# Decoder layer in f32 on one core: each full weight chunk is requested as two transfers of 512 KB instead of one of 1 MB

## The chip, the cores and the metric

The kernel runs on one core of a Trainium2 chip. The metric is the device time of one execution in microseconds (us), as the median of several executions. The kernel before took 1955.75 us (three executions, 1953.15 to 1957.33 us).

The core has five engines that run their own instruction streams side by side: TensorE (PE in the profile; PEld is its weight load), VectorE (DVE), ScalarE (ACT), GpSimd (POOL) and SyncE (SP), which here only asks for transfers. Each engine takes its instructions in the order in which they were placed, and waits at an instruction until the semaphores that it names have been reached. A transfer is issued by an instruction on an engine's queue (SP's queue is SPq in the profile), is carried out by 16 DMA engines, and reports its landing on a semaphore.

## The reference

One decoder layer on 256 tokens of width 2048, batch 1, everything in float32:

```python
hn = rmsnorm(h, norm_mix_w[l])
q, k, v, g_ret, xr, yr, g_a, g_b = jnp.split(hn @ w_in[l], offsets, axis=-1)
...
ret_out = jax.nn.silu(g_ret) * ret          # retention, 8 heads, rotary, head norm
rnn_out = jax.nn.gelu(yr) * hr              # causal conv of 4 taps, gated recurrence
merged = (jax.nn.sigmoid(g_a) * (ret_out @ w_proj_ret[l])
          + jax.nn.sigmoid(g_b) * (rnn_out @ w_proj_rnn[l]))
h = h + merged @ w_mix_out[l]
hn = rmsnorm(h, norm_xa_w[l])
mem_n = rmsnorm(mem, norm_mem_w[l])
h = h + memory_cross_attention(hn, mem_n, xa_w_q[l], xa_w_k[l], xa_w_v[l], xa_w_o[l])
hn = rmsnorm(h, norm_ffn_w[l])
h = h + conv_gated_ffn(hn, ffn_w_up[l], ffn_conv_w[l], ffn_conv_b[l], ffn_w_down[l])
return rmsnorm(h, final_norm_w)
```

Nearly all of the work is in the products with the weight matrices: `w_in` is 2048 x 14336, seven more (both mixers' outputs, the merge, and four of the cross-attention) are 2048 x 2048, `ffn_w_up` is 2048 x 11264 and `ffn_w_down` is 5632 x 2048. Each weight is used once for the 256 tokens, so all of them have to be read from the chip's memory once per execution.

## The kernel before

**Products.** A float32 product is made of three products in the reduced type fp32r: a number is split into a high part (its value cast to fp32r) and a low part (the rest), and high x high, high x low and low x high are added up. So each weight has to be split on the chip. ScalarE casts (`hi`, line 451) and VectorE subtracts (`lo`, line 452), both in `weight_parts`, for two pieces of 128 x 512 at a time (`KH` = 2). TensorE then multiplies (line 285, every product of the kernel goes through this helper). The activations are the stationary operand, and the weights are streamed past them.

**Chunks.** The weights lie in one array `wall` in the order in which they are used, packed by the host so that what one partition needs of a chunk is contiguous. A full chunk is four pieces, 128 x 2048 numbers, 1 MB, 8 KB for each of the 128 partitions. There are two sorts of them that matter here:

- plain chunks: `for k in range(0, nk, KH): parts += weight_parts(raw[:, one])`. The first cast reads pieces 0 and 1, the second reads pieces 2 and 3.
- seven-part chunks (`seven_parts`, line 466): two column blocks are multiplied with seven products in the place of eight, from sums and differences of the four pieces. Their first cast reads `raw[:, 0:3:2]`, pieces 0 and 2, and their second reads piece 3. Line 473 then makes three sums over the pieces in place (VectorE), and two more pairs of casts and subtractions follow.

**Staging.** A generator (`chunks`) hands out the chunks in order and calls `prefetch` ahead of use (`AHEAD` = 2). `prefetch` takes the next entry of the stream, takes a tile `raw` of the pool with `RAW_BUFS` = 3 slots of 1 MB, asks for the load on SP's queue (line 416, which calls `load`, whose transfer is recorded as line 256), and lists the casts and subtractions. `hi` and `lo` have `PART_BUFS` = 6 slots of two pieces each, three chunks' worth. A load into a `raw` slot waits until the chunk three earlier has been read for the last time, which is a `lo` subtraction on VectorE.

Some chunks take other ways: the first six (small, at the start), those whose low part is made by a DMA that adds (`fr`, `fl`), and those of which a part comes in as `tw`.

**Order.** A scheduler places the instructions of all engines by priorities and its own estimates of durations; TensorE's products are held in program order (`keep_in_program_order`). SP's queue carries, beside the weight loads, 128 transposes by DMA (line 665 in `by_dma`, `pt<-pl`). For them ScalarE first splits rows into two planes (`pl`, line 664), and later joins the turned planes (`f`, line 677). On SP's queue a load that stands behind transposes is issued after them.

**Names that the text uses.** `raw`: a loaded chunk. `pl`, `pt`, `f`: planes before and after the turn, and the joined rows. `acc`, `sm`: sums in PSUM, `o`: sums that VectorE carries on (lines 627 and 638). `s`, `ts`: split activations. `fg`, `fv`, `ft`, `fo`: gate, value and their product in the FFN (lines 1280, 1282, 1290, 1291).

Of the kernel before, what the change touches and what calls it, by code (L numbers as in the profile page):

```python
# [30 lines left out]
KH = 2  # L31
# [168 lines left out]
def hybrid_layer(  # L200
# [155 lines left out]
    def prefetch(n):  # L356
        while len(ahead) < n and taken[0] < len(stream):
            i = taken[0]
            name, row, nk, c = stream[i]
# [48 lines left out]
            k2 = row // (KH * P)  # L408
            early = i < 2 * len(EARLY)
            own = early and i % 2 == 0  # L410
            cuts = () if i == 0 else range(0, nk + 1, KH) if i < 6 else (0, nk)
            if own:
                xs.load(k2 + 1)
            for a, b in zip(cuts, cuts[1:]):
# [69 lines left out]
    def chunks(nk, w, row, c):  # L484

        i = gemms[0]
        assert plan[i] == (w, row, nk, c), (i, w, row, nk, c)
        gemms[0] += 1
        for k, n in pieces(i, nk, c):
            prefetch(1)  # L490
            (r_, c_), parts = ahead.pop(0)
            assert (r_, c_) == (row + k * P, kind_of(c, k))
            prefetch(AHEAD)
            yield k, n, parts
            step[0] += 1
            due = [p for p in pending if p[0] <= step[0]]
            pending[:] = [p for p in pending if p[0] > step[0]]
            for _, fn in due:
                fn()
# [981 lines left out]
```

## Time and profile before

| what | value |
|---|---|
| median of three executions | 1955.75 us (1953.15 to 1957.33) |
| the profiled execution, its own time | 1956.59 us |
| span in its trace, first to last instruction | 1954.5 us |
| instructions on all engines in the trace | 24287 |
| TensorE clock granted, mean | 0.999 |
| weight loads of 1 MB on SP's queue | 319 |
| weight loads of 768 KB / of 512 KB into `raw` | 24 / 13 |
| transposes on SP's queue | 128 |
| DMA traffic | 454.99 MB, mean 233 GB/s |

The span is the time on the core, and the execution's own time is 2.1 us more. A row of the timeline names the start and the length of a run of like instructions, the engine, the line, and the tile written and read (`hi<-raw`). Its length goes from the first's start to the last's end. Instructions that only issue a transfer are not counted as busy work of an engine, but the queue's own rows (SPq) show how long each issue held the queue. "us to landing" counts from the issue to the semaphore that reports the transfer.

### The profile page before, as it was taken

To read this page: it belongs to the slowest core of one execution; us is meant where nothing else is said; L and a number is where in the kernel's file an instruction comes from. 1 tells how busy PE (TensorE), PEld (TensorE's weight loads), DVE (VectorE), ACT (ScalarE), POOL (GpSimd) and SP (SyncE) were. 2 spreads that over 40 slices of the span, in tenths; PEclk is the share of its full clock that TensorE was granted. 3 is DMA by queue.
4 is the path that set the end of the run, shared out by engine and by line. 5 is a ranking of instruction groups with operands and counts; after the bars stand their busy time and mean duration, and the time that the engine had idled before them with its cause. 6 is when DMAs were issued, how large, how long until landed. Compare 5 with 4: busy or idle time off the path is not lost.

```text
span 1954.5 us, 24287 instructions
## 1 busy us (share of the span) xinstructions
PE 1944.4 (99%) x8735; PEld 1612.9 (83%) x8735; DVE 1659.0 (85%) x2155; ACT 1457.7 (75%) x1792; POOL 68.5 (4%) x69
## 2 busy tenths in 40 slices
PE   9999999999999999999999999999999999999998
PEld 7888888888888888888888888888887888888887
DVE  6887987787889988887888857789999889999986
ACT  6665758999756666778678777888877578884784
POOL 0000001000100000000000000000000000000000
PEclk9999999999999999999999999999999999999999
DMA  8866767666867786778868687676677877678773
GB/s 332 262 215 198 245 222 217 213 218 229 237 217 265 233 264 215 253 253 252 247 213 239 223 221 225 226 232 226 211 224 224 269 248 221 223 224 271 230 255 119
DMA packets 211352, 454.99 MB, mean 233 GB/s; under 512 B 143264, under 2 KB 147872, under 8 KB 170400
## 3 DMA queue, kind: packets, MB, share of 16 engines
q1 hardware_dynamic: 204896, 430.38, 66.5%
q0 software_dynamic: 6336, 23.07, 6.3%
q8 instruction: 68, 1.11, 0.2%
q14 instruction: 52, 0.43, 0.1%
HBM read 407.27 MB, written 2.10 MB: 209 GB/s over the span
## 4 chain that ended last, share of the span: by engine, by line
PE 88%; DVE 5%; ACT 3%; DMA 2%; issue 2%; POOL 0%; SPq 0%; POOLq 0%; DVEq 0%; ACTq 0%
PE acc L285 63%; PE sm L285 26%; DVE lo L452 2%; ACT hi L451 1%; DMA raw<-in_wall 1%; ACT f L677 1%; DVE o L627 1%; ACT pl L664 0%; DMA fl<-fr 0%; DVE o L638 0%; DMA pt<-pl 0%; DVE raw L473 0%; DVE fv L1282 0%; DVE fg L1282 0%; DVE s L702 0%
## 5 line engine op out<-in xcount | busy, mean ns | idle before, releaser
L452 DVE TENSOR_TENSOR lo<-raw,hi 128x1024 fp32r<-128x1024 f32 (+1 forms) x824 | 940.4, 1169 | 203.0 <-ACT hi L451 193.0
L285 PE MATMUL acc<-hi,s 128*128 128x512 f32 x3526 | 1081.5, 388 | 0.4 <-ACT s L727 0.2
L451 ACT CAST hi<-raw 128x1024 fp32r<-128x1024 f32 (+1 forms) x824 | 801.1, 1007 | 301.9 <-DMA raw<-in_wall 83.1
L285 PEld LDWEIGHTS acc<-hi,s 128*128 128x128 f32 x3526 | 659.5, 188 | 136.1 <-DVE s L728 0.6
L285 PE MATMUL acc<-lo,s 128*128 128x512 f32 x1727 | 669.7, 388 | 0.1
L285 PE MATMUL sm<-hi,s 128*128 128x512 f32 x1464 | 450.9, 389 | 0.0
L285 PEld LDWEIGHTS acc<-lo,s 128*128 128x128 f32 x1727 | 324.4, 188 | 68.6 <-DVE lo L452 2.1
L285 PEld LDWEIGHTS sm<-hi,s 128*128 128x128 f32 x1464 | 274.7, 188 | 57.2 <-ACT prob L1203 0.2
L285 PE MATMUL sm<-lo,s 128*128 128x512 f32 x720 | 280.3, 389 | 0.0
L677 ACT COPY f<-pt 128x1024 uint16<-128x1024 uint16 x128 | 166.8, 1353 | 10.0 <-DMA pt<-pl 10.0
L285 PEld LDWEIGHTS sm<-lo,s 128*128 128x128 f32 x720 | 135.2, 188 | 28.6 <-DVE lo L452 0.6
L285 PE MATMUL acc<-hi,ts 128*128 128x512 f32 x438 | 134.9, 389 | 0.0
L473 DVE TENSOR_TENSOR raw<-raw 128x1024 f32<-128x1024 f32 x147 | 127.1, 865 | 1.9
L285 PEld LDWEIGHTS acc<-hi,ts 128*128 128x128 f32 x438 | 82.2, 188 | 17.0
L285 PE MATMUL acc<-lo,ts 128*128 128x512 f32 x219 | 85.7, 391 | 0.7 <-DVE lo L452 0.6
L664 ACT COPY pl<-o 128x1024 uint16<-128x1024 uint16 x64 | 62.5, 1040 | 3.7 <-DVE o L638 2.8
L330 POOL DMA_DIRECT2D tw<-in_wall x24 | 21.4, 891 | 980.8 <-DMA tw<-in_wall 355.7
L285 PEld LDWEIGHTS acc<-lo,ts 128*128 128x128 f32 x219 | 41.1, 188 | 10.8 <-DVE lo L452 2.4
L664 ACT COPY pl<-rows 128x1024 uint16<-128x1024 uint16 x44 | 43.7, 1044 | 7.6 <-DVE rows L694 7.6
L1421 ACT ACTIVATE o<-o,ro 128x512 f32<-128x512 f32 x44 | 30.1, 718 | 23.9 <-DVE o L638 23.8
L638 DVE TENSOR_TENSOR o<-o,sm 128x512 f32<-128x512 f32 x64 | 42.2, 679 | 3.9 <-PE sm L285 3.9
L285 PE MATMUL sm<-hi,ts 128*128 128x512 f32 x146 | 45.0, 389 | 0.0
(197 smaller groups left out, 1321.2 us busy)
## 6 DMA issues: line engine op xcount, KB each, us to landing
raw<-in_wall SPq DMA_DIRECT2D x319, 1024.0 KB, 5.1
raw<-in_wall SPq DMA_DIRECT2D x24, 768.0 KB, 5.6
tw<-in_wall SPq DMA_DIRECT2D x24, 512.0 KB, 7.7
tw<-in_wall POOLq DMA_DIRECT2D x24, 512.0 KB, 7.3
raw<-in_wall SPq DMA_DIRECT2D x13, 512.0 KB, 6.6
fr<-in_wall SPq DMA_DIRECT2D x12, 512.0 KB, 7.4
fl<-fr POOLq DMA_DIRECT2D x12, 512.0 KB, 8.1
nat<-in_x SPq DMA_DIRECT2D x8, 512.0 KB, 9.7
```

Of the source, the lines that this page charges most:

```text
L285: tc.keep_in_program_order(pe.matmul(*a, **k))
L330: pool.dma_start(out=far[i], in_=source(i)[:, 0:KH, :], accum_op=ALU.add)
L451: act.copy(hi[:, cs], src[:, cs])
L452: dve.tensor_tensor(out=lo[:, cs], in0=src[:, cs], in1=hi[:, cs].bitcast(F32), op=ALU.subtract)
L473: dve.tensor_tensor(out=o, in0=a, in1=b, op=ALU.add)
L627: dve.tensor_tensor(out=o, in0=a, in1=b, op=op)
L638: dve.tensor_tensor(out=o, in0=o, in1=a, op=ALU.add)
L664: act.copy(planes[:, tt], words[:, tt])
L677: act.copy(halves_[:, :, :, cs], turned_[:, :, :, cs])
L1421: act.mul(a[:, tt, :], a[:, tt, :], rs2[:, tt : tt + 1])
```

## The change

```diff
@@ prefetch
-            cuts = () if i == 0 else range(0, nk + 1, KH) if i < 6 else (0, nk)
+            cuts = () if i == 0 else range(0, nk + 1, KH)
             if own:
                 xs.load(k2 + 1)
             for a, b in zip(cuts, cuts[1:]):
                 with tc.issue_after(behind[-1]) if i in in_order else nullcontext():
                     load(raw[:, a:b, :], src[:, a:b, :], early)
```

`cuts` are the pieces at which a chunk's load is cut. From the seventh entry of the stream on they were (0, 4), and are now 0, 2, 4 as for the first ones: pieces 0 and 1 in one transfer, pieces 2 and 3 in a second one, into the two halves of the same tile, 4 KB for each partition in each. The bytes, the tiles, the casts and the products are the same. On SP's queue there are 885 transfer instructions in the place of 566, 319 more. PE's and POOL's order is the same row for row. The scheduler places some rows of the others differently; all but 20 of the pairs stand back to back on SP's queue. Three places follow. Numbers in names differ between the two kernels, since names are counted through.

SP's queue in the FFN, at chunk A, a seven-part chunk (`raw_13903` before, `raw_14168` now). Before:

```order
L256 DMA raw_13869<-in_wall 128x2048
L256 DMA raw_13903<-in_wall 128x2048
L665 DMA_TRANSPOSE pt_13806<-pl_13805 128x8x128 x2
L665 DMA_TRANSPOSE pt_13814<-pl_13813 128x8x128 x2
L256 DMA raw_13956<-in_wall 128x2048
```

Now:

```order
L256 DMA raw_14133<-in_wall 128x1024 x2
L256 DMA raw_14168<-in_wall 128x1024
L665 DMA_TRANSPOSE pt_14070<-pl_14069 128x8x128 x2
L665 DMA_TRANSPOSE pt_14078<-pl_14077 128x8x128 x2
L256 DMA raw_14168<-in_wall 128x1024
L256 DMA raw_14222<-in_wall 128x1024 x2
```

The load of A stood whole ahead of the four transposes. Its first half still does; its second half stands behind them. Eight chunks on, at chunk B (`raw_14264` before, `raw_14537` now, also of seven parts), SP's queue has the same pattern.

ScalarE at chunk B (`f` and `fg` are the FFN's joined rows and gate, `ft` its activation). Before:

```order
L451 CAST hi_14266<-raw_14264 128x1024
L677 COPY f_14309<-pt_14178 128x2x4x128
L451 CAST hi_14270<-raw_14264 128x512
L677 COPY f_14309<-pt_14178 128x2x4x128
L1280 ACTIVATE fg_13819<-f_14309,pf 128x256 x2
L451 CAST hi_14277<-raw_14264 128x1024
L1280 ACTIVATE fg_13819<-f_14309,pf 128x256 x2
L677 COPY f_14402<-pt_14186 128x2x4x128
L451 CAST hi_14281<-raw_14264 128x1024
```

Now:

```order
L677 COPY f_14583<-pt_14449 128x2x4x128 x2
L1280 ACTIVATE fg_14083<-f_14583,pf 128x256 x3
L451 CAST hi_14540<-raw_14537 128x1024
L451 CAST hi_14544<-raw_14537 128x512
L1280 ACTIVATE fg_14083<-f_14583,pf 128x256
L677 COPY f_14678<-pt_14457 128x2x4x128 x2
L1290 ACTIVATE ft_14687<-fg_14083 128x512
L451 CAST hi_14551<-raw_14537 128x1024
L1280 ACTIVATE fv_14084<-f_14678,pf 128x256 x2
L451 CAST hi_14555<-raw_14537 128x1024
```

The two joins of `f` and three of the gate's rows moved ahead of B's first cast, and the joins of the next planes and `ft` ahead of its third.

VectorE at chunk C, a plain chunk of the FFN (`raw_12362` before, `raw_12595` now). Before:

```order
L1282 SCALAR_TENSOR_TENSOR fv_11711<-f_12295,pf,fv_11711 128x254
L452 TENSOR_TENSOR lo_12365<-raw_12362,hi_12364 128x1024
L638 TENSOR_TENSOR o_12343<-o_12343,sm_12085 128x512
L1291 TENSOR_TENSOR fo_12356<-ft_12355,fv_11711 128x512
L638 TENSOR_TENSOR o_12343<-o_12343,sm_12086 128x512
L452 TENSOR_TENSOR lo_12369<-raw_12362,hi_12368 128x1024
```

Now:

```order
L1282 SCALAR_TENSOR_TENSOR fv_11930<-f_12527,pf,fv_11930 128x254
L638 TENSOR_TENSOR o_12576<-o_12576,sm_12312 128x512
L638 TENSOR_TENSOR o_12576<-o_12576,sm_12313 128x512
L1291 TENSOR_TENSOR fo_12589<-ft_12588,fv_11930 128x512
L452 TENSOR_TENSOR lo_12599<-raw_12595,hi_12598 128x1024
L452 TENSOR_TENSOR lo_12603<-raw_12595,hi_12602 128x1024
```

C's first subtraction stood ahead of two sums of `o` and the product `fo`, and now stands behind all three.

## The prediction

> **What bounds the kernel now.** I read the page first: the shares of the engines, the DMA queue, and the chain that ended last.
>
> ```profile
> span 1954.5 us, 24287 instructions
> PE 1944.4 (99%) x8735; PEld 1612.9 (83%) x8735; DVE 1659.0 (85%) x2155; ACT 1457.7 (75%) x1792; POOL 68.5 (4%) x69
> q1 hardware_dynamic: 204896, 430.38, 66.5%
> PE 88%; DVE 5%; ACT 3%; DMA 2%; issue 2%; POOL 0%; SPq 0%; POOLq 0%; DVEq 0%; ACTq 0%
> ```
>
> TensorE is busy in 1944.4 of 1954.5 us, and the loads fill the 16 DMA engines to 66.5%. Then the busy time by stretches, to see where TensorE's missing 10.1 us lie. The columns are the length, then for PE, PEld, DVE, ACT and POOL the busy time with the number of instructions, then clock, DMA share and GB/s.
>
> ```profile
> 0.00:14.00 14.00, 12.71 (x49) 9.88 (x50) 7.54 (x17) 8.00 (x15) 0.97 (x7) 1.00 0.84 299
> 14.00:1420.00 1406.00, 1405.24 (x6341) 1167.99 (x6340) 1177.29 (x1527) 1066.71 (x1313) 53.02 (x44) 1.00 0.73 234
> 1420.00:1540.00 120.00, 119.15 (x518) 96.42 (x517) 108.06 (x137) 86.92 (x106) 3.52 (x4) 1.00 0.77 240
> 1540.00:1946.00 406.00, 406.00 (x1822) 337.55 (x1822) 363.87 (x469) 294.90 (x360) 10.43 (x13) 1.00 0.71 228
> 1946.00:1954.50 8.50, 1.32 (x12) 1.11 (x10) 2.26 (x7) 1.12 (x2) 0.54 (x1) 0.85 0.35 135
> ```
>
> The start (1.29 us, with chunks that the change leaves as they are) and the tail (7.18 us, after the last product) hold 8.47 us of it. Between them, in 1932 us, TensorE stands still for 0.76 + 0.85 + 0.00 = 1.61 us. So an earlier load has next to nothing to win, and whatever holds TensorE up once is paid in full. The question is whether TensorE is ever made to wait, and this hangs on the staging ahead of it. The waits, by who waited for whom (total us, times, longest):
>
> ```profile
> ACT hi L451 <- DMA raw<-in_wall: 83.1, 63, 5.7
> ACT hi L451 <- PE acc L285: 77.6, 73, 3.1
> ACT hi L451 <- PE sm L285: 57.5, 61, 1.9
> SPq L256 <- DVE lo L452: 1209.9, 300, 11.9
> PE acc L285 <- DVE lo L452: 0.6, 2, 0.4
> ```
>
> ScalarE waits for a load 63 times and for TensorE (to free a `hi`) 134 times, while TensorE waited only twice, for 0.6 us, for a subtraction. The staging is ahead nearly everywhere, by little. SP's queue waits 1209.9 us for VectorE to free a `raw` slot.
>
> **The change part by part.** *The 319 further issues.* The first row gives what one issue holds the queue (least, median, most, in ns); the others are page rows and single issues in the trace (KB, us to landing).
>
> ```profile
> L256 SPq DMA_DIRECT2D raw<-in_wall x356: 327/328/1059, 1.7 to 1917.7; - x178
> raw<-in_wall SPq DMA_DIRECT2D x319, 1024.0 KB, 5.1
> raw<-in_wall SPq DMA_DIRECT2D x13, 512.0 KB, 6.6
> raw<-in_wall SPq DMA_DIRECT2D x1, 512.0 KB, 3.1
> raw<-in_wall SPq DMA_DIRECT2D x1, 1024.0 KB, 4.7
> raw<-in_wall SPq DMA_DIRECT2D x2, 1024.0 KB, 6.0
> ```
>
> 319 x 0.33 = 105 us of SP's time, in a queue that waits 1209.9 us for slots: hidden where nothing urgent stands behind it. Without that cover it would delay the second half by 0.33 us per chunk, and ScalarE's wait with it.
>
> *Landing.* The third and second rows from the end are one load of 512 KB (issued at 523.0) and one of 1 MB (1631.7), each without another weight load in flight: 3.1 and 4.7 us. (The last row is two loads asked for between 1684.2 and 1685.4, of use further down.) So a first half lands up to 1.6 us sooner, and a second half, issued 0.33 us later, at about the old time. The median over 13 loads of 512 KB (they come amid other transfers) is 6.6 us, more than the 5.1 us of the full ones, so neither order of sizes is safe: I bound a half's landing by 3.1 and 6.6 us and take 4.0 us amid transposes, nearer the lone row. For plain chunks, whose first cast needs the first half only, part of the 83.1 us of ScalarE's waits goes. TensorE gets from it at most its own pauses. A pause looks shorter in busy time than it is, since a product is counted 0.39 us but the next one starts 0.23 us after it; I double the 1.61 us: a gain between 0 and 3.2 us. I take 0.5, as TensorE's waits in the list end at VectorE.
>
> [...]
>
> *Chunk A.* Its second half now stands behind four transposes on SP's queue. Before (start, length):
>
> ```profile
> 1635.19 0.33 SPq L256 DMA_DIRECT2D raw<-in_wall  x1
> 1635.57 8.36 SPq L665 DMA_TRANSPOSE pt<-pl  x4
> 1644.03 1.68 SPq L256 DMA_DIRECT2D raw<-in_wall  x2
> ...
> 1639.30 4.42 ACT L451 CAST hi<-raw 128x1024 fp32r<-128x1024 f32 x5 [0.28 <-DVE raw L337]
> 1647.73 1.04 ACT L451 CAST hi<-raw 128x1024 fp32r<-128x1024 f32 x1
> ...
> 1645.53 1.22 DVE L473 TENSOR_TENSOR raw<-raw 128x1024 f32<-128x1024 f32 x1
> 1648.87 1.22 DVE L452 TENSOR_TENSOR lo<-raw,hi 128x1024 fp32r<-128x1024 f32 x1
> ...
> 1652.93 0.62 PE L285 MATMUL acc<-hi,ts 128*128 128x512 f32 x2
> 1653.38 0.39 PE L285 MATMUL acc<-lo,ts 128*128 128x512 f32 x1
> ```
>
> The half is issued at 1635.57 + 8.36 = 1643.9 in the place of 1635.2, and lands at 1647.9 (1647.0 to 1650.5). A is of seven parts, so its first cast needs both halves: it moves from about 1642 (the fourth of the five casts at 1639.30) to 1647.9. From there the order is cast (1.04 us), subtraction and the three sums of line 473. Before, 3.3 us lay between the first sum's start (1645.53) and the third subtraction's (1648.87). First subtraction at about 1648.9, first sum some 1.8 us later at 1650.7, third subtraction at 1654.0, done at 1655.2. TensorE reads it at 1653.38: **1.8 us late, I take 2** (0 by the early landing and the sums closer together, 4 by the late one).
>
> *Chunk B*, the same pattern eight chunks on, and the chunk behind it:
>
> ```profile
> 1676.18 0.33 SPq L256 DMA_DIRECT2D raw<-in_wall  x1
> 1676.56 7.63 SPq L665 DMA_TRANSPOSE pt<-pl  x4
> ...
> 1681.70 1.05 ACT L451 CAST hi<-raw 128x1024 fp32r<-128x1024 f32 x1 [0.38 <-DMA raw<-in_wall]
> 1692.63 1.04 ACT L451 CAST hi<-raw 128x1024 fp32r<-128x1024 f32 x1
> ...
> 1700.63 3.50 DVE L452 TENSOR_TENSOR lo<-raw,hi 128x1024 fp32r<-128x1024 f32 x3
> ...
> 1702.34 0.39 PE L285 MATMUL acc<-lo,ts 128*128 128x512 f32 x1
> ```
>
> The second half is issued at 1684.2 and lands at 1688.2, so B's first cast moves by 6.5 us from 1681.70. The new order on ScalarE (shown with the change) uses part of that time: both joins and three gate rows stand ahead of it now. What is left between B's first cast and the next chunk's (10.9 us before) I add up at 7.9 us, so the next chunk's first cast starts at 1696.1 in the place of 1692.63, 3.5 us late. It had no spare time: its fourth subtraction, at 1700.63, was done at 1701.8 for a product at 1702.34. Some VectorE rows (`fv`) no longer stand between, worth about 1 us, and 0.5 us was spare: **2 us** (0 to 4; should the transposes' own delays shift PE's need by A's stall, less).
>
> *Chunk C* moves by the scheduler alone. Its first subtraction now stands behind two sums and `fo`:
>
> ```profile
> 1458.47 1.21 DVE L452 TENSOR_TENSOR lo<-raw,hi 128x1024 fp32r<-128x1024 f32 x1
> 1459.61 0.68 DVE L638 TENSOR_TENSOR o<-o,sm 128x512 f32<-128x512 f32 x1
> ...
> 1461.41 1.21 DVE L452 TENSOR_TENSOR lo<-raw,hi 128x1024 fp32r<-128x1024 f32 x1
> ...
> 1458.99 0.61 PE L285 MATMUL acc<-hi,s 128*128 128x512 f32 x2
> 1459.74 0.50 PE L285 MATMUL acc<-lo,s 128*128 128x512 f32 x1
> ```
>
> The three rows took 1461.41 - 1459.61 = 1.80 us. TensorE was already waiting for this subtraction: two products further on it starts 0.75 us after 1458.99, where two rows above (1652.93 to 1653.38) it takes 0.45. So nearly all 1.8 us reach it; the subtractions behind it are then less pressed, which may give back some of the pauses after it. **1.5 us** (0 to 1.9).
>
> *The other 18 pairs that are pulled apart*, and rows moved by a few places on ScalarE and VectorE. Most pairs stand in stretches where ScalarE waits for TensorE, with spare time of some us; a plain chunk needs its second half only for its second cast. Each could cost between nothing and A's 4 us. **1 us** for all (0 to 6).
>
> The sum against the profiled execution's own 1956.6 us: 2 + 2 + 1.5 + 1 - 0.5 = +6.0, so 1962.6. That execution lies 0.8 us above the median of the three shown; against the median, **1962 us**. The bounds add to -3.2 and +16, not all likely at once.
>
> **The rivals.** *One: nothing of it reaches TensorE* (not slower). The mechanism is the spare time at A, B and C: if the second halves land 3.1 us after issue, with the sums of line 473 following at once, A's third subtraction is done in time, and the scheduler's other moves give back at C what they take. For it: TensorE's two short waits in the old trace and the 134 times at which ScalarE waits for it. It decides once the delays at A and B stay below 6 us together with the shorter work between. Against it: the spare time of 0.5 us behind B and of none at C. It gives 1955 to 1958 us. *Two: faster,* by the earlier first halves alone: TensorE's pauses of up to 3.2 us go and A to C cost nothing, 1956.6 - 3.2 - 0.8 = 1952.6 us. For it, ScalarE's 63 waits for loads and VectorE's waits behind them; against it, C's pause, which ends at VectorE's row above it. *Three: the two halves of a chunk follow each other instead of overlapping,* so that a chunk takes 2 x 3.1 = 6.2 us in the place of 4.7. ScalarE's 63 waits for loads grow by 1.5 us each, 95 us, of which I let a quarter reach TensorE, as it has spare time at most places: +24, 1980 us. Against it: two full loads asked for within 1.2 us landed after 6.0 us (the median of both), where in turn the second would have needed some 9. *Four: more of the 18 pairs than I think strike,* at 2 us each for five of them: +10, some 1970 us.
>
> **How the numbers follow.** A measurement of this kernel tells about 0.2% from no change, 3.9 us: faster means below 1951.8, slower above 1959.7. My forecast (delays at A, B, C, +4 to +8) has a chance of 0.50, rival one 0.22, two 0.12, three 0.05, four 0.11. Rival two lies 0.8 us above the border and the three runs shown lie 4 us apart, so faster gets half of it, 0.06; the same gets one, the other half of two and 0.06 of the forecast whose stalls fall short, 0.34; slower the rest, 0.44 + 0.05 + 0.11 = 0.60. For the range, 8 in 10: from 1954, which takes in rival one and leaves out two, to 1971, which takes in most of rival four and leaves out three. The forecast's own range is 1959 to 1966.
>
> **What would show it.** In the new trace: transfers of 512 KB, some 640 of them, and landings of about 3 to 4 us. At A, SP's queue holds the four transposes between two issues of `raw`, and TensorE pauses about 2 us, in the timeline some 18 us after the first half's issue, ending at `lo<-raw`. After B a second such pause ends at `lo`; at C one of 1.5 us. TensorE's waits for `lo` rise from 0.6 to 5 or 6 us, and nothing ends at a DMA directly. The sum of ScalarE's waits for `raw` may fall for the plain chunks. I would be wrong if TensorE's idle time stays below 3 us outside start and tail, if it pauses at many chunks whose halves stand back to back (rival three), or if the largest pauses lie at pairs that I did not price.

## The result: 1972.05 us, 0.85% slower, and the profile after

| | median | ratio to the kernel before |
|---|---|---|
| before, beside it | 1955.12 us (1953.15 to 1957.33, 4 runs) | |
| both halves asked for apart | 1972.05 us (1970.71 to 1972.73, 4 runs) | 1.0085 (95% interval 1.0072 to 1.0098) |
| predicted | 1962.0 us (range 1954 to 1971) | |

The direction was right and the size was not: 17 us in the place of 6, and just outside the range. The page of the kernel after, the rows that answer to those shown of before:

```profile
span 1970.8 us, 24888 instructions
PE 1949.9 (99%) x8735; PEld 1612.3 (82%) x8735; DVE 1658.6 (84%) x2155; ACT 1457.7 (74%) x1792; POOL 70.0 (4%) x69
q1 hardware_dynamic: 250832, 430.40, 68.5%
raw<-in_wall SPq DMA_DIRECT2D x651, 512.0 KB, 4.9
```

The five engines have as many instructions as before, and the DMA engines are 2 points busier, with 45,936 further packets. A half lands after 4.9 us by the median, a whole load after 5.1. Busy time by stretches, with the same columns as before:

```profile
14.00:1420.00 1406.00, 1401.95 (x6318) 1162.79 (x6317) 1170.83 (x1516) 1060.89 (x1305) 54.50 (x44) 1.00 0.76 233
1420.00:1540.00 120.00, 117.66 (x518) 96.42 (x517) 108.11 (x141) 87.51 (x108) 3.52 (x4) 1.00 0.75 226
1540.00:1962.20 422.20, 416.22 (x1845) 341.94 (x1844) 369.01 (x475) 299.23 (x363) 10.47 (x13) 1.00 0.72 223
```

TensorE's idle time between start and tail has grown from 1.61 to 4.05 + 2.34 + 5.98 = 12.37 us. That is 10.8 of the 16.3 us by which the span has grown. Its busy time has grown by 5.5 us as well (1944.4 to 1949.9): part of each pause is counted as busy, as the prediction said (a product is counted 0.39 us, and the next one starts 0.23 us after it), and some products ran slowly (0.43 us apart in 1711-1715, last section). The waits say for whom:

```profile
PE acc L285 <- DVE lo L452: 7.7, 10, 1.3
PE acc L285 <- DMA fl<-fr: 1.2, 1, 1.2
PE acc L285 <- ACT hi L451: 1.0, 2, 0.8
ACT hi L451 <- DMA raw<-in_wall: 85.5, 80, 6.2
SPq L256 <- DVE lo L452: 1066.6, 299, 11.4
```

TensorE waits for subtractions, 7.7 us in the place of 0.6, and at ten places in the place of two.

TensorE's 8735 products stand in the same order in every kernel of this document. So the start of each product can be set against that of the same product before, and the difference shows where a kernel falls behind. The table gives what TensorE lost in each stretch (us, by the times of the old trace; A lies in 1640-1668, B in 1668-1735, C in 1440-1520). There is one trace of each kernel. Where two rows have the same order and the same split in a stretch they still differ, mostly by about 1 us and at most by 1.8 (500-940 in the changed kernel and e9, C in e10 and e16), so smaller differences say nothing.

| run | 14-500 | 500-940 | 940-1440 | C | 1520-1640 | A | B | 1735-1947 |
|---|---|---|---|---|---|---|---|---|
| the changed kernel | +0.8 | +3.8 | +0.9 | -0.5 | +0.8 | +0.5 | +6.2 | +4.3 |
| split, old order (e1) | 0.0 | -0.2 | +0.7 | -0.1 | +1.6 | 0.0 | +0.3 | +0.6 |
| whole loads, new order (e2) | +0.8 | +7.7 | +1.1 | -0.3 | +0.1 | +3.1 | +6.8 | +1.4 |
| new order, halves together (e3) | +0.5 | +4.2 | +1.3 | +2.7 | -0.7 | 0.0 | +5.5 | 0.0 |
| new order, B's stretch old (e9) | +0.5 | +5.6 | +1.0 | +0.2 | +0.8 | +0.5 | +1.8 | +3.3 |
| old order, B's stretch new (e10) | 0.0 | -1.0 | +0.1 | +0.3 | +1.3 | 0.0 | +4.6 | +0.2 |
| new order up to 1000 us (e11) | +0.5 | +4.5 | +1.0 | +0.8 | +0.6 | 0.0 | +0.1 | +0.8 |
| old order, B's half late (e13) | 0.0 | -0.7 | -0.1 | -0.5 | +1.9 | 0.0 | +5.8 | 0.0 |
| old order, A's half late (e16) | 0.0 | -0.5 | -0.1 | -1.5 | +1.2 | +2.6 | +1.0 | 0.0 |
| old order, C's stretch new (e17) | 0.0 | +0.1 | -0.1 | -1.0 | +2.1 | 0.0 | +0.4 | 0.0 |
| needed pieces first, old order (e18) | 0.0 | +0.4 | -0.1 | -2.2 | -0.7 | 0.0 | +1.1 | 0.0 |

14.3 of the changed kernel's 16.8 us lie in three stretches. Of these the prediction had priced B by itself alone, at a third.

### The profile page after: what moved, and what is told of

Same layout as the page of the kernel before. It is cut to its first block, busy times and chain, and to the rows that moved or that the text cites. A ratio compares the mean times of both kernels' runs of the same rounds, so it can differ in the third digit from the quotient of the medians.

```text
span 1970.8 us, 24888 instructions
## 1 busy us (share of the span) xinstructions
PE 1949.9 (99%) x8735; PEld 1612.3 (82%) x8735; DVE 1658.6 (84%) x2155; ACT 1457.7 (74%) x1792; POOL 70.0 (4%) x69
## 4 chain that ended last, share of the span: by engine, by line
PE 85%; DVE 7%; ACT 3%; issue 2%; DMA 2%; POOL 0%; SPq 0%; DVEq 0%; POOLq 0%; ACTq 0%
PE acc L285 60%; PE sm L285 26%; DVE lo L452 3%; ACT hi L451 1%; DMA raw<-in_wall 1%; DVE raw L473 1%; DVE o L627 1%; DVE o L638 0%; ACT pl L664 0%; DMA fl<-fr 0%; ACT f L677 0%; DVE fv L1282 0%; DMA pt<-pl 0%; DVE fo L1291 0%; DVE fg L1282 0%
## 5 line engine op out<-in xcount | busy, mean ns | idle before, releaser
L451 ACT CAST hi<-raw 128x1024 fp32r<-128x1024 f32 (+1 forms) x824 | 802.8, 1008 | 323.0 <-DMA raw<-in_wall 85.5
L1282 DVE SCALAR_TENSOR_TENSOR fg<-f,pf,fg 128x255 f32<-128x255 f32 (+1 forms) x88 | 40.3, 481 | 6.6 <-ACT fg L1280 6.1
```

What stands on the lines that cost most here:

```text
L451: act.copy(hi[:, cs], src[:, cs])
L1282: dve.scalar_tensor_tensor(out=y[:, s:S], in0=z[:, j, 0 : S - s], scalar=pf[:, 2 - s, t : t + 1], in1=y[:, s:S], op0=ALU.mult, op1=ALU.add,)
```

## The experiments: the order apart from the split

An order can be held fixed. A scheduler normally places the instructions; here a table gives each engine's whole order instead, as offsets from the order in which the program lists them, and each instruction is tied behind its forerunner on its engine. The ties hold neighbours of one engine together and should add no wait; e15 below, with all tables of before and 49 loads split, is level with the kernel before (1.0002). So a split can be run in the old order and whole loads in the new one. "Old order" means the order of the kernel before, with the two halves where the whole load stood.

```diff
     with tile.TileContext(nc) as tc:
         hybrid_layer(tc, *args)
+        in_order_of(nc, tc)
...
+def in_order_of(nc, tc):
+    traced = {}
+    for i in nc.cur_bb.bb.instructions:
+        if type(i).__name__ != "BassTilePoolBoundary":
+            traced.setdefault(str(i.engine).split(".")[-1], []).append(i)
+    edge = mybir.DependencyInfo(mybir.DependencyClass.NoSync, mybir.DependencyReason.DATA)
+    for engine, table in ORDER.items():
+        off = np.frombuffer(zlib.decompress(base64.b85decode(table)), np.int16)
+        line = [traced[engine][k + int(d)] for k, d in enumerate(off)]
+        for a, b in zip(line, line[1:]):
+            tc.add_manual_dep(b, a.name, edge, reason="order")
```

In what follows an edit is this table and, where named, the line `cuts`. A result is given as the median, the ratio to the kernel before on the same chip with its 95% interval, and where useful what the ratio makes of 1955 us. Expectations name absolute times; differences between two runs are taken from the ratios, as the runs come from three chips.

**Split, old order (e1).** Edit: `cuts` as in the change, all tables of the kernel before.

> All 319 loads are split, but every queue keeps the order of the kernel before: each pair stands where the whole load stood, its halves one behind the other, and ScalarE, VectorE and GpSimd have their old order. Theory 'placement' (the 16 us come from where the scheduler now puts halves, casts and subtractions): within 3 us of the kernel before, 1953 to 1958 us. Rival 'transfers' (twice as many transfers, each with its own cost, semaphore and packets): most of the 17 us stays, 1966 to 1972 us. Between 1959 and 1965 both have a share.

Measured: 1958.87 us, 1.0018 (1.0009 to 1.0027), +3.5 us. Some 13 of the 17 us go with the order alone. The split keeps a small share; the time lies 0.9 us above the range of "placement".

**Whole loads, new order (e2).** Edit: `cuts` as before, the changed kernel's tables, a whole load at its first half's place.

> Whole loads of 1 MB as before, but ScalarE, VectorE and GpSimd in the order of the changed kernel, and each load at the place where its first half stands there. Theory 'placement': the moved casts and subtractions cost without any split; the sums pulled ahead at C and the joins pulled ahead at B remain, the late halves do not: 1958 to 1966 us. Rival 'transfers': no loss without a split, 1953 to 1958 us.

Measured: 1979.69 us, 1.0122 (1.0108 to 1.0136), +24 us, outside both forecasts. The new order costs without any split, and more without it than with it.

**New order, halves together (e3).** Edit: the changed kernel's tables, the 20 late second halves moved up behind their first halves.

> The changed kernel with its own order on ScalarE, VectorE and GpSimd, but the 20 second halves that stood behind something else on SyncE's queue now stand directly behind their first halves. Its distance to the changed kernel is the price of late halves, its distance to the run with whole loads in the new order is the price of the transfers. Theory 'placement': late halves make up more than half, so 1958 to 1964 us, and as fast as whole loads in the new order to within 2 us. Rival 'transfers': 1966 to 1972 us, and over 8 us slower than whole loads in that order.

Measured: 1970.18 us, 1.0072 (1.0060 to 1.0085), +14 us. Late halves on SyncE's queue are worth 2 to 3 us net, hardly clear of the scatter, and not more than half. "Transfers" named this time, but for another reason: in this order the split is 9.5 us faster than whole loads, where it forecast over 8 us slower. It may be that this order counts on a first half that lands early, which a whole load doesn't give; that isn't shown. What is left for the 14 us is the order: on ScalarE and VectorE, and at nine places on SyncE's queue, where set against e1 a load or a transpose has another place. The table shows the same: 4.2 us in 500-940 and 5.5 us at B stay with the halves together. But the 2 to 3 us are a sum of gains and losses. 1735-1947 got better by 4.3 us, all that was lost there, so there the late halves were the price (more on this below). C got worse by 3.2 us: TensorE waits 2.97 us for the subtraction there, and its granted clock is 0.72 in 1466-1472.

How an order costs is seen at a seven-part chunk in 860-875, chunk D. ScalarE in the timeline of the kernel before (start, length, operation), and VectorE's row of D's third subtraction:

```profile
859.38 1.04 ACT L451 CAST hi<-raw 128x1024 fp32r<-128x1024 f32 x1
860.32 1.36 ACT L677 COPY f<-pt 128x1024 uint16<-128x1024 uint16 x1
...
862.16 1.03 ACT L451 CAST hi<-raw 128x1024 fp32r<-128x1024 f32 x1
863.10 0.50 ACT L727 ACTIVATE s<-f,pb 128x256 fp32r<-128x256 f32 x1
863.51 1.55 ACT L451 CAST hi<-raw 128x1024 fp32r<-128x1024 f32 x2
...
869.67 1.23 DVE L452 TENSOR_TENSOR lo<-raw,hi 128x1024 fp32r<-128x1024 f32 x1
```

The same place in the changed kernel, which is 2.5 us behind there, with the same row of VectorE and TensorE's row:

```profile
860.47 2.57 ACT L677 COPY f<-pt 128x1024 uint16<-128x1024 uint16 x2
862.90 1.04 ACT L451 CAST hi<-raw 128x1024 fp32r<-128x1024 f32 x1
863.84 1.71 ACT L727 ACTIVATE s<-f,pb 128x256 fp32r<-128x256 f32 x4
...
866.40 1.36 ACT L677 COPY f<-pt 128x1024 uint16<-128x1024 uint16 x1
867.62 1.56 ACT L451 CAST hi<-raw 128x1024 fp32r<-128x1024 f32 x2
...
873.57 1.22 DVE L452 TENSOR_TENSOR lo<-raw,hi 128x1024 fp32r<-128x1024 f32 x1
...
874.84 0.50 PE L285 MATMUL acc<-lo,ts 128*128 128x512 f32 x1 [0.82 <-DVE lo L452]
```

Four rows of `s` in the place of one, and a join more, stand ahead of D's first pair of casts. They start at 867.62 in the place of 863.51, 4.1 us later where TensorE is 2.5 us later, and TensorE waits for the chunk's third subtraction, which starts 3.9 us later. No single move is large: a join is 1.36 us, a row of `s` 0.4. It costs because the staging there was ahead by less than that: before, the third subtraction was done at 870.90 for a product at 871.35, 0.45 us ahead. With the halves together (e3) TensorE still loses 1.1 us at this product, as in the changed kernel (1.0).

**Around B.** Edit of e9: the changed kernel's tables, but from five chunks ahead of B to five behind it the old ones. Of e10: the reverse, the old tables with the new ones in that stretch.

> The changed kernel, but in the stretch around chunk B (five chunks ahead of it to five behind) SyncE, ScalarE and VectorE have their old order, halves together; everywhere else the changed kernel's order. Theory 'places' (the loss is a sum of stalls at single places, each set by the order there): the 6 us that TensorE lost around B go, 1964 to 1967 us. Rival 'spread' (the staging runs thinner everywhere, and a stall taken away at B comes back a little later): 1970 to 1973 us.

> The reverse: all loads split in the old order of every queue, but in the stretch around chunk B the changed kernel's order on SyncE, ScalarE and VectorE, with B's late half. Theory 'places': some 6 us more than the split loads in the old order (1958.9 us): 1963 to 1967 us, with TensorE's stalls right behind B. Rival 'spread': B is only where a shortage from further back shows: 1957 to 1961 us.

Measured: e9 1967.47 us, 1.0054 (1.0040 to 1.0068), 6 us less than the changed kernel by the ratios (4.6 by the medians), a little above the expected range; its trace loses 1.8 us at B in the place of 6.2. e10 1962.28 us, 1.0034 (1.0022 to 1.0047), 3 us more than the split in the old order and 0.7 below the expected range; its trace loses 4.6 us at B. Both say "places", at some three quarters of the price. The stretch doesn't always cost the same: in the changed kernel 1.6 of the 6.2 us go by a slower clock (last section), which e10 doesn't have.

**B's late half alone (e13), A's late half alone (e16).** Edit: the old tables, with SyncE's order of the changed kernel around B, or around A.

> All loads split in the old order, but on SyncE's queue alone the stretch around B as in the changed kernel: B's second half stands behind four transposes, with the old order on ScalarE and VectorE. Theory 'late half' (as predicted: B's first cast waits for it, and the next chunk has no spare time): 2 to 4 us more than 1958.9 us, so 1961 to 1963 us, and more than half of what the whole stretch costs. Rival 'order of casts' (the joins and gate rows that stand ahead of B's casts are the price): within 1.5 us of 1958.9 us.

> All loads split in the old order, but A's second half stands behind the four transposes on SyncE's queue, with the old order on ScalarE and VectorE. As predicted, A's third subtraction comes 2 us late: 1960 to 1962 us (1958.9 + 2, bounds 0 to 4). Rival 'spare time' (as in the changed kernel, where A cost next to nothing): 1958 to 1959.5 us. Since B's half alone cost 4 us with the old casts, as much is possible here: up to 1963 us.

Measured: e13 1963.03 us, 1.0036 (1.0023 to 1.0048), 3.5 us more than e1, "late half"; TensorE loses 5.8 us at B. e16 1961.24 us, 1.0031 (1.0019 to 1.0043), 2.5 us more than e1, as predicted; TensorE loses 2.6 us at A. Both intervals overlap with that of e1, and the trace of e16 is that of its fastest execution (1957.68 us), so the places in the table are the better evidence. With the old casts, late halves cost about what the prediction said for A, and more for B: 3.5 us by the times and 5.8 by the trace, in the place of 2. But the changed kernel doesn't have the old casts: there the joins stand ahead of B's casts, which uses the time and by itself costs as much (e3: 5.5 us at B with the halves together, some 1.1 of them, by estimate, by a slower clock, 0.86 in 1712-1720). The prices of the two don't add up.

**The first part alone (e11).** Edit: the changed kernel's tables up to the 180th chunk, the old ones behind it.

> All loads split; the changed kernel's order on all queues up to the 180th chunk (some 1000 us), and the old order behind it. Theory 'places': the 4 us that TensorE lost in this part and no more, 1962 to 1965 us (1958.9 + 4). Rival 'spread': a late stream stays late and costs behind this point too, 1966 us or more.

Measured: 1963.06 us, 1.0035 (1.0022 to 1.0048), as "places" expected. TensorE stays 4.5 us late and doesn't fall further behind than the split in the old order does.

**C (e17).** Edit: the old tables, with the new ones of ScalarE and VectorE around C.

> All loads split in the old order, but around chunk C ScalarE and VectorE have the changed kernel's order, with C's first subtraction behind two sums and a product; SyncE's order is the old one. As predicted, 1.5 us: 1959.5 to 1961 us, with a pause at C and smaller pauses in the 40 us behind it. Rival 'given back': TensorE is late by 1 us at C and makes it up at the pauses behind, 1958 to 1959.4 us.

Measured: 1957.42 us, 1.0015 (1.0006 to 1.0024), no more than e1: the rival, though 0.6 us below its range. TensorE falls 0.5 us behind at C and is 1.5 us further ahead by 1520. Kernels with the old order at C gain there too (e16 1.5, e18 2.2 us), so that C is made up is shown, and by which rows is not.

**Plain chunks alone, seven-part chunks alone.** Edits:

```diff
-            cuts = () if i == 0 else range(0, nk + 1, KH)
+            cuts = () if i == 0 else (0, nk) if i >= 6 and isinstance(c, tuple) and c[2] == 1 else range(0, nk + 1, KH)
```

for the plain ones, and with `not (...)` around the condition on `c` for the seven-part ones. e5 and e6 are placed by the scheduler, e14 and e15 have the old order. (270 of the 319 loads are plain chunks, not 172 as the first expectation says.)

> Only plain chunks are split; the seven-part chunks, whose first cast needs both halves, are loaded whole again, and the scheduler places everything itself. Theory 'placement by way of seven-part chunks' (a late half costs where the first cast needs it): the stalls of A, B and the chunk behind B go, at least 6 of the 16 us: 1955 to 1964 us. Rival 'transfers': about 172 of 319 pairs remain, so about half the loss remains at places all over the run, 1962 to 1966 us, with no large pauses.

> Only the 49 seven-part chunks are split, and the scheduler places everything itself. Theory 'late halves of seven-part chunks make the order worse': most of the 17 us, 1966 to 1973 us. Rival 'any disturbance of the old order': the two partial splits share the loss, 1959 to 1965 us; 17 us less the 5 us of the plain ones alone would be 1967 us if the two add up.

> Old order of every queue; only the 270 plain chunks are split, the 49 seven-part chunks are loaded whole. Theory 'both halves needed' (the 3.5 us that a split costs in the old order arise where a seven-part chunk's first cast needs the second half, which is issued and lands later): 1953 to 1956.5 us, as before or better, since plain chunks' first halves land sooner. Rival 'each transfer costs': 270 of 319 parts of 3.5 us remain, 1957.5 to 1959 us.

> Old order of every queue; only the 49 seven-part chunks are split. Theory 'both halves needed': all of the 3.5 us of the split in the old order, 1957.5 to 1959.5 us. Rival 'all together' (only when all 319 loads are split is SyncE's queue full enough to hurt): 1954 to 1956.5 us.

| | scheduler's order | old order |
|---|---|---|
| plain chunks split | e5: 1959.94 us, 1.0026 (1.0016 to 1.0037) | e14: 1955.87 us, 1.0004 (0.9995 to 1.0012) |
| seven-part chunks split | e6: 1960.79 us, 1.0035 (1.0022 to 1.0049) | e15: 1955.39 us, 1.0002 (0.9993 to 1.0011) |
| all split | the changed kernel: 1.0085 | e1: 1958.87 us, 1.0018 (1.0009 to 1.0027) |

In the old order neither part of the split costs anything that can be measured alone; both together cost 3.5 us (the interval of e1 just touches those of e14 and e15). So "both halves needed" as I put it for e15 fell, though e14 came out as it said; e15 fits the rival "all together". In the scheduler's order each part of the split costs 5 to 7 us, e6 as "any disturbance of the old order" expected. For e5 the time came out as "by way of seven-part chunks" expected, but e14 shows that its 5 us are the order's too.

**The needed pieces first (e18, e20).** Edit, e18 in the old order, e20 placed by the scheduler:

```diff
-                    load(raw[:, a:b, :], src[:, a:b, :], early)
+                    ks = slice(a // KH, nk, KH) if i >= 6 and isinstance(c, tuple) and c[2] == 1 else slice(a, b)
+                    load(raw[:, ks, :], src[:, ks, :], early)
```

> Old order of every queue, all 319 loads split, but the seven-part chunks are cut into pieces 0 and 2 in the first transfer and pieces 1 and 3 in the second, so that the first cast needs the first transfer only. Theory 'both halves needed': the 3.5 us go, 1954 to 1956.5 us. Rival 'second transfer late for the second cast or the sums anyway': 1957.5 to 1960 us.

> All 319 loads split, seven-part chunks into pieces 0 and 2 and pieces 1 and 3 as in the run before, but with everything placed by the scheduler. Theory 'any new order is worse': 1962 to 1972 us. Rival 'late halves made the order bad': with the first cast no longer in need of the second half, 1953 to 1958 us.

Measured: e18 1953.76 us, 0.9993 (0.9984 to 1.0001): the 3.5 us of e1 are gone, as "both halves needed" expected (0.2 us below its range), and the kernel is level with the one before, not surely faster. e20 1963.25 us, 1.0046 (1.0032 to 1.0060), as "any new order is worse" expected: another order by the scheduler, another 9 us. With e14, e15, e18 and e1 against e5, e6, e20 and the changed kernel, the old order was better four times out of four, by 4 to 13 us.

Where e1 loses is seen at one place in 1520-1640, the stretch in which it loses most. SyncE asks for two seven-part chunks one behind the other, and ScalarE's first cast of the first of them waits. Before (the middle row is that chunk's load, with KB and us to landing):

```profile
1510.57 2.56 SPq L256 DMA_DIRECT2D raw<-in_wall  x2
raw<-in_wall SPq DMA_DIRECT2D x1, 1024.0 KB, 8.3
1518.96 1.05 ACT L451 CAST hi<-raw 128x1024 fp32r<-128x1024 f32 x1 [5.67 <-DMA raw<-in_wall]
```

All split, old order (e1), with the rows of both halves of that chunk and TensorE's next wait:

```profile
1510.40 4.24 SPq L256 DMA_DIRECT2D raw<-in_wall  x4
raw<-in_wall SPq DMA_DIRECT2D x1, 512.0 KB, 8.2
raw<-in_wall SPq DMA_DIRECT2D x1, 512.0 KB, 9.0
1519.85 1.05 ACT L451 CAST hi<-raw 128x1024 fp32r<-128x1024 f32 x1 [6.79 <-DMA raw<-in_wall]
1533.76 0.50 PE L285 MATMUL acc<-lo,ts 128*128 128x512 f32 x1 [1.17 <-DVE lo L452]
```

All split, needed pieces first (e18; the cast stands one line further down in that kernel):

```profile
1507.20 4.41 SPq L256 DMA_DIRECT2D raw<-in_wall  x4
1515.37 1.05 ACT L452 CAST hi<-raw 128x1024 fp32r<-128x1024 f32 x1 [5.66 <-DMA raw<-in_wall]
```

From the first issue to the cast it takes 8.39 us before, 9.45 in e1 and 8.17 in e18. (The rows of SPq also hold the time until the second chunk's slot is free.) In e1 the second half is issued 0.38 us after the first and takes 9.0 us to land, so that the cast, which needs both, comes 1.1 us later. Where the first cast has what it needs in the first transfer, this is gone. At TensorE's wait e1 loses 0.8 us against the kernel before, and so do e10, e13, e16 and e17, which split this chunk in the same way; e14, which loads it whole, and e18 don't. That is 0.8 of the 3.5 us. Where the rest arises isn't shown.

**Cut by partitions (e12).** Edit, in the old order: each chunk as two transfers of 64 partitions with 8 KB each.

```diff
-                    load(raw[:, a:b, :], src[:, a:b, :], early)
+                    ps = slice(a // KH * P // 2, (a // KH + 1) * P // 2)
+                    load(raw[ps, 0:nk, :], src[ps, 0:nk, :], early)
```

(The first chunks are left as they were.)

> Two transfers of 512 KB per chunk in the old order of every queue, but cut by partitions (64 partitions with 8 KB each, twice) instead of by pieces (128 partitions with 4 KB each). As many transfers as in the split by pieces, rows as long as before. Now every chunk needs both halves for its first cast. Theory 'second transfer' (its own issue on SyncE's queue and its later landing are the price): no better than the split by pieces, 1957 to 1962 us. Rival 'short rows' (4 KB in the place of 8 KB for each partition): back at the kernel before, 1954 to 1956.5 us.

Measured: 2197.64 us, 1.1233 (1.1218 to 1.1248), far outside both. The pages of e1, cut by pieces in the same order, and then of this run:

```profile
span 1956.9 us, 24915 instructions
q1 hardware_dynamic: 250832, 430.40, 68.6%
...
span 2196.3 us, 25068 instructions
q1 hardware_dynamic: 210000, 430.40, 88.6%
raw<-in_wall SPq DMA_DIRECT2D x651, 512.0 KB, 8.3
```

It can't tell short rows from second transfers, since it brought a larger cost of its own: the same bytes in rows of 8 KB fill the DMA engines to 88.6% of a longer span, 1946 us in the place of 1342, and a half lands after 8.3 us (4.8 in e1).

ScalarE's and VectorE's orders weren't tried apart, and neither were late halves for all 20 pairs in the old order of casts.

## Why the prediction was right in its sign and wrong in its size

- **What bounds the kernel: right.** TensorE paid nearly every stall in full, and none was made up later except at C. e11 shows it most plainly (4.5 us lost in 500-940, and none of it back by 1947).
- **The 319 issues "hidden": nearly right.** The median issue went from 0.33 to 0.41 us, and SyncE still waits 1066.6 us for slots. But "a second half at about the old time" doesn't hold everywhere: at 1510 in e1 it lands 9.4 us after the first issue, where the whole load took 8.3. In the old order the whole split costs 3.5 us, where the prediction gained 0.5.
- **Landing: right.** 4.9 us by the median over all, in the range of 3.1 to 6.6. ScalarE's waits for loads fell in the old order (83.1 to 63.8 us in e1), as forecast for plain chunks; in the new order they didn't (85.5 us).
- **Chunk A, 2 us: the mechanism holds alone, and hardly shows in the changed kernel.** Alone the late half costs 2.6 us (e16). In the changed kernel A's stretch costs 0.5 us. SyncE and ScalarE there, and SyncE in e16:

```profile
1640.63 6.05 SPq L665 DMA_TRANSPOSE pt<-pl  x4
1646.73 3.89 SPq L256 DMA_DIRECT2D raw<-in_wall  x5
...
1650.20 1.57 ACT L451 CAST hi<-raw 128x1024 fp32r<-128x1024 f32 x2 [0.39 <-DMA raw<-in_wall]
```

```profile
1634.40 5.84 SPq L665 DMA_TRANSPOSE pt<-pl  x4
```

  The transposes hold the queue for 6.05 us, not 8.36, and the half lands 3.4 us after its issue, not 4.0. The first cast is 3 us late by TensorE's measure (5 us behind at this place, and the old cast at some 1642.2), where I had 6. The shorter transposes alone don't explain the small loss: in e16 they took 5.84 us, and the first cast still came 4.4 us late and cost its 2.6 us. The order of ScalarE's rows differs too; why A came off so lightly in the changed kernel is open.
- **Chunk B, 2 us (0 to 4): mis-sized, 6.2 us.** The late half does what was foretold, and more:

```profile
1685.86 5.36 SPq L665 DMA_TRANSPOSE pt<-pl  x4
1691.27 2.47 SPq L256 DMA_DIRECT2D raw<-in_wall  x5
...
1695.69 1.57 ACT L451 CAST hi<-raw 128x1024 fp32r<-128x1024 f32 x2 [1.97 <-issue]
1702.54 2.01 ACT L451 CAST hi<-raw 128x1024 fp32r<-128x1024 f32 x2
```

  TensorE is 5.7 us behind at this place. B's first cast comes 8.3 us late beside it (forecast 6.5), the next chunk's first cast, the second of the two at 1702.54, about 5 us late (forecast 3.5). TensorE stood still five times on the way. Against the old trace it falls 1.8 us behind at three products of B itself, which the term left out, 2.6 us at two of the chunk behind (forecast 2, at its fourth subtraction; measured at its third cast and subtraction), and 1.6 us while its clock is down (last section).
- **Chunk C, 1.5 us: 0.** At C itself the three rows cost 1.1 us in the changed kernel and 0.5 in e17, but by 1520 the "may give back" was all of it.
- **"The other 18 pairs that are pulled apart, and rows moved by a few places on ScalarE and VectorE. ... 1 us for all (0 to 6)": the step that failed.** What it covers is the changed kernel's loss in the stretches without A, B and C: 0.8 + 3.8 + 0.9 + 0.8 + 4.3 = 10.6 us in the place of 1. Both parts of the term were too small. *The moved rows:* I read the order for late halves on SyncE's queue and priced the casts' order at nothing much, by the argument that ScalarE has spare time of some us. The spare time was there on the average, not at the places where rows moved. The 3.8 us in 500-940 stay with the halves together (e3: 4.2); D shows one of the places. *The late halves:* nearly all of the 4.3 us in 1735-1947 lie behind two of the 18 pairs, both of plain chunks with a second half behind four transposes. TensorE falls 1.7 us behind after the first (a pause of 1.25 us at 1756.55) and 2.5 us after the second, and with the halves together (e3) this stretch loses 0.0. The second one, in the changed kernel and then in e3:

```profile
1900.63 7.78 SPq L665 DMA_TRANSPOSE pt<-pl  x4
1915.86 1.05 ACT L451 CAST hi<-raw 128x1024 fp32r<-128x1024 f32 x1 [3.30 <-DMA raw<-in_wall]
...
1930.97 0.50 PE L285 MATMUL acc<-hi,s 128*128 128x512 f32 x1 [0.94 <-ACT s L701]
```

```profile
1911.67 1.04 ACT L451 CAST hi<-raw 128x1024 fp32r<-128x1024 f32 x1
```

  The chunk's second cast waits 3.30 us for the half, and the rows behind it on ScalarE, `s` among them, come late for TensorE; in e3 the same cast doesn't wait. "Needs its second half only for its second cast" was true of this chunk, and not enough.
- **The rivals.** Rival four gave 1970 us, near the result, by five of the 18 pairs at 2 us each. Two of them struck, at 1.7 and 2.5 us; the rest of the loss is the order, since e3, with all halves together, is only 2 to 3 us faster. So its number came near by luck, and its mechanism held in part. The sign "if the largest pauses lie at pairs that I did not price" came true in part as well. Rival three (halves in turn) fell with e14, e15 and e18, where a split costs nothing that can be measured. Rival two's gain is 1.4 us in e18 (the interval reaches from a gain of 3.1 us to none).
- **What stays open.** Why the scheduler's orders for split loads are 4 to 13 us worse than its order for whole loads isn't settled: its estimates of landings weren't looked at. Whether ScalarE's order carries the loss, or VectorE's, or the nine moved rows on SyncE's queue have a share, is open too.

## What to carry to other kernels

Where a scheduler places instructions, a change of transfers is two changes: the transfer and the new order. Run the transfer in the old order (and the old transfer in the new order) before judging either; here the order, late halves included, held 13 of 17 us. In this kernel, whose one engine is 99% busy, a move of one or two rows of 1 us cost TensorE time where the staging was ahead by less than that, so read the spare time at each moved row, not as an average. And when a load is cut, cut it so that the first consumer has all it needs in the first part: in the old order this was the difference between e18 and e1, 5 us.

## What the runs showed of the hardware that I had not expected

**Half the partitions.** In e12 the loads' queue kept the DMA engines busy for 0.886 x 2196.3 = 1946 us, in e1 for 0.686 x 1956.9 = 1342 us: transfers of 512 KB to 64 partitions took 1.45 times the engines' time of those to 128 partitions, for the same bytes and longer rows. (The queue carries the transposes too. If those took as long in both, the factor for these loads alone is larger, by estimate.) The kernel took 1.1233 times as long as the one before. Loads cut into 512 KB by pieces, over 128 partitions, changed the kernel's time by -0.1 to +0.2% as long as the order stayed (ratios of 1.0004 in e14, 1.0002 in e15, 0.9993 in e18 and 1.0018 in e1), with the DMA engines at 68.6% in e1.

**A slower clock after two pauses.** After two pauses near B (0.76 and 1.26 us), TensorE's clock fell in the changed kernel. Its rows, then the windows around:

```profile
1710.91 0.50 PE L285 MATMUL acc<-lo,ts 128*128 128x512 f32 x1 [1.26 <-DVE lo L452]
...
1713.06 0.63 PE L285 MATMUL acc<-lo,ts 128*128 128x512 f32 x1
1713.49 1.06 PE L285 MATMUL acc<-hi,s 128*128 128x512 f32 x2
```

```profile
1709.00:1711.00 2.00, 0.74 (x3) 0.30 (x3) 2.00 (x4) 1.19 (x2) 0.00 (x0) 1.00 0.15 59
1711.00:1715.00 4.00, 4.00 (x11) 3.16 (x12) 4.00 (x6) 3.64 (x4) 0.00 (x0) 0.57 0.40 128
```

The granted clock is 0.57 in 1711-1715 and the products start 0.43 us apart in the place of 0.23. In the trace's record of the clock it stands at 0.5 for 3.4 us there. Set against the old trace TensorE falls 1.6 us further behind meanwhile, a quarter of B's 6.2. The longest of TensorE's pauses near B is 1.26 us. The clock doesn't fall at each such pause: e10, with the same order around B and pauses of 0.77 and 1.26 us at the same two products, kept a granted clock of 1.00 in every window of 1690-1720 and lost 4.6 us. So did e13, with pauses of 0.5 us at most and 5.8 us lost. What brought the clock down isn't shown.
